# Top-k logits four heads at a time on alternating halves of the array's rows, products with values on alternating column halves

## Chip, cores and metric

The kernel runs on one core of a Trainium2 chip. The metric is device time in microseconds (us) of one execution, as the median of several runs.

## What is computed

A trunk of two layers on 256 tokens of width 1024. A layer is a root-mean-square norm, a wide projection, two attention mixers side by side (8 heads each of 64 for the top-k mixer, 4 pairs of heads for the differential one), a projection back, and a SwiGLU block. Cut to what matters here:

```python
qa, ka, va, iq, ik, iw, qb, kb, vb = split(rms_norm(x) @ w_in)
# top-k mixer: each query keeps the 64 keys with the best index score
score = sum_h relu(iq_h . ik) * iw_h ;  idx = top_k(score, 64)
logits = qa_h . ka_h[idx] / 8 ;  out_a = softmax(logits) @ va_h[idx]      # 8 heads
# differential mixer
p = softmax(qb_hc . kb_hc / 8) ;  out_b = rms_norm((p_0 - lam * p_1) @ vb_h)  # 4 heads, c = 0, 1
x = x + concat(out_a, out_b) @ w_out
x = x + (silu(h2 @ w_gate) * (h2 @ w_up)) @ w_down
```

A query sees only keys of its own and earlier chunks of 64, so the first 128 queries (block 0) see 128 keys and the second 128 (block 1) see 256.

## The kernel before, in words

Tokens lie in two blocks of 128. Each large product is made of three products of float32r parts (`mm3`, lines 193 to 199: activations' hi by weights' hi, lo by hi, hi by lo). The weights come by DMA as `wraw` and are split on chip: ScalarE (ACT) casts `whi` (line 174), VectorE (DVE) subtracts to `wlo` (line 175). Activations are split the same way: `split_psum` casts `hi` on ACT (L303, or L306 with a gain) and makes `lo` on DVE (L304, L307).

The order of TensorE (PE) is written out by the class `Weave`. There is one main stream of large products: seven groups of the projection (idx, qb, kb, vb, qa, ka, va), then `wo`, then gate, up and down. Beside it run threads of small work, generators that yield a delay and a list of events. `small_mm`, `transpose` and `mm3` add an estimated time to `W.now` (`W.spend`), and a thread goes on in front of the main stream once its delay has passed and its events are there. So an estimate that changes moves all that is planned after it. The other engines' order is set by the tile scheduler, which follows program order and readiness. PSUM is eight banks, taken in turn.

The threads that matter here: `attn_b` (diff mixer; logits `lg_b`, transposed probabilities `ppt_b` and `pT_b`, output `ob`, its norm `subln` that ends in `pt_mb`, `hi_mb`, `lo_mb`), `attn_a` (top-k mixer; `lg_a`, `ppt_a`, `pT_a`) and `pv_a` (products with values, output `po`, split to `hi_ma`, `lo_ma`). `wo` reads first `hi_mb`, `lo_mb` of both blocks, then `hi_ma`, `lo_ma`.

A head's query and key have 64 rows, so a logit matmul takes half of the array's rows: even heads the rows 0 to 63, odd heads 64 to 127. `softmax_pair` does two heads of one half into one bank: two matmuls, on DVE a masked row-maximum for each head (L479), on ACT the exponential (L482), on DVE the reciprocal of the sums (L485). `attn_a` asks for pairs (0, 2), (1, 3), (4, 6), (5, 7) of a block, up to three ahead of the transposes; `attn_b` calls it twice in a row, for the two pairs of an item. An output `po` is 64 columns of values by 128 queries, so its matmul takes half of the array's columns; block 1 adds two key tiles.

Of the kernel before, what the change touches and what calls it, by code (L numbers as in the profile page):

```python
# [17 lines left out]
P = 128  # L18
D = 1024
S = 256  # L20
# [28 lines left out]
class Weave:  # L49
    """Orders the tensor engine's work: one main stream of large products, and threads of small  # L50
    ones, each of which says how long (in estimated microseconds) its operands take to be ready."""

# [56 lines left out]
def tile_hybrid_trunk(ctx, tc, x, w_in, w_out, vecs, w_gate, w_up, w_down, g_final, rope, out):  # L109
# [10 lines left out]

    # ---------------------------------------------------------------- weight stream
    NSUB = 1024
# [81 lines left out]

    # ---------------------------------------------------------------- inputs that stay
    LAMROW = 2 * DEPTH * KT + DEPTH
# [28 lines left out]

    # gains and lambda vectors, one per column
    gT = pool.tile([P, ROWS], F32, tag="gT", name="gT")
# [57 lines left out]
    def split_psum(pt, name, scales=None, tag="act", bufs=12):  # L295
        """Columns of a bank as hi and lo tiles; scales: one factor per partition for each of them."""
        n = pt.shape[1]
        tags = tag if isinstance(tag, tuple) else (tag, tag)
        bufs = bufs if isinstance(bufs, list) else [bufs, bufs]
        hi = pool.tile([P, 4, P], F32R, tag=tags[0], bufs=bufs[0], name=f"hi_{name}")  # L300
        lo = pool.tile([P, 4, P], F32R, tag=tags[1], bufs=bufs[1], name=f"lo_{name}")
        if scales is None:
            nc.scalar.copy(hi[:, :n], pt)  # L303
            nc.vector.tensor_tensor(lo[:, :n], pt, hi[:, :n].bitcast(F32), op=ALU.subtract)  # L304
        elif len(scales) == 1:
            nc.scalar.activation(hi[:, :n], pt, AF.Copy, scale=scales[0])  # L306
            nc.vector.scalar_tensor_tensor(lo[:, :n], pt, scales[0], hi[:, :n].bitcast(F32),  # L307
                                           op0=ALU.mult, op1=ALU.subtract)
        else:
            sc = pool.tile([P, 4, P], F32, tag="hff", bufs=3, name=f"sc_{name}")  # L310
            for k in range(0, n, 2):
                scaled(sc, pt, scales, k, k + 2)
                hilo(sc, hi, lo, k, k + 2)
        return [(hi[:, k], lo[:, k]) for k in range(n)]
# [32 lines left out]
    def norm(kind, L, b, h):  # L347
        """One half of the transposes of x, scaled by the gain (the row factor is applied to the products)."""
        yield DN, ()
        norm_T(kind, L, b, h)  # L350
        norm_split(kind, L, b, h)
        if h == 1:
            rstd[kind, L, b] = norm_rstd(b, f"{kind}{L}{b}")

    # ---------------------------------------------------------------- what follows a projection
    T = {}

    def matT(t, o, name):
        """[tokens, 512] -> [128, 4, tokens], float32."""
        pt = bank(f"ptq_{name}").rearrange("p (k t) -> p k t", k=4)  # L360
        for k in range(4):
            transpose(pt[:, k], t[:, k * P:(k + 1) * P])
        nc.scalar.copy(o, pt)
# [17 lines left out]
    def after_proj(L, nm, b, ps):  # L381
        name = f"{nm}{L}{b}"
        r = rstd["mix", L, b]
        if nm == "idx":
# [5 lines left out]
            nc.vector.tensor_tensor(t.rearrange("p h d -> p (h d)"), a[:, :288], c[:, :288], op=ALU.add)  # L390
            # hi and lo side by side: (hi, lo, hi, lo) of a query meets (hi, hi, lo, lo) of a key
            sq = pool.tile([P, 8, 4, 32], F32R, tag=("kbT", "kaT")[b], bufs=1, name=f"ixq{L}{b}")
# [36 lines left out]

    # ---------------------------------------------------------------- attention  # L430
    def small_mm(cost, *a, **k):
        nc.tensor.matmul(*a, **k)  # L432
        W.spend(cost)
# [32 lines left out]

    def softmax_pair(L, b, q, k, mask, pair, name):
        """Unnormalized probabilities of two heads of one row group, and one over their sums."""
        nk = (b + 1) * P
        ps = bank(f"lg_{name}").rearrange("p (i k) -> p i k", i=2)  # L470
        for i, h in enumerate(pair):
            rws = slice(64 * (h % 2), 64 * (h % 2) + 64)
            small_mm(0.213 * (b + 1), ps[:, i, :nk], T[q, b][rws, h // 2, :], T[k][rws, h // 2, :nk],
                     start=True, stop=True)
        p = pool.tile([P, 2, S], F32, tag="prob", bufs=5, name=f"p_{name}")
        mx = small(2, f"mx_{name}")
        sm = small(2, f"sm_{name}")
        for i in range(2):
            nc.vector.tensor_tensor_reduce(out=p[:, i, :nk], in0=ps[:, i, :nk], in1=mask[:, :nk], scale=-0.125,  # L479
                                           scalar=3.0e38, op0=ALU.add, op1=ALU.min, accum_out=mx[:, i:i + 1])  # L480
        for i in range(2):
            nc.scalar.activation(p[:, i, :nk], p[:, i, :nk], AF.Exp, scale=-1.0, bias=mx[:, i:i + 1],  # L482
                                 accum_out=sm[:, i:i + 1])
        rc = small(2, f"rc_{name}")
        nc.vector.reciprocal(rc, sm)  # L485
        return p, rc

# [9 lines left out]
    def attn_b(L):  # L497
# [5 lines left out]
        def qk(b, hp):  # L503
            nk = (b + 1) * P
            p0, r0 = softmax_pair(L, b, "qb", "kb", smask[:, b], (4 * hp, 4 * hp + 2), f"b{L}{b}{hp}0")
            p1, r1 = softmax_pair(L, b, "qb", "kb", smask[:, b], (4 * hp + 1, 4 * hp + 3), f"b{L}{b}{hp}1")
            nl = small(2, f"nl{L}{b}{hp}")
            nc.vector.tensor_scalar(nl, r1, neglam[:, L:L + 1], None, op0=ALU.mult)
            for i in range(2):
                nc.scalar.activation(p1[:, i, :nk], p1[:, i, :nk], AF.Copy, scale=nl[:, i:i + 1])  # L510
                nc.vector.scalar_tensor_tensor(p0[:, i, :nk], p0[:, i, :nk], r0[:, i:i + 1], p1[:, i, :nk],
                                               op0=ALU.mult, op1=ALU.add)
            prob[b, hp] = p0
            ready[b, hp] = W.now + DB[b]
# [41 lines left out]
    def attn_a(L):  # L556
        items = [(b, n) for b in range(NB) for n in range(4)]
        ready, prob, pTs = {}, {}, {}

        def qk(b, n):  # L560
            nk = (b + 1) * P
            p, rc = softmax_pair(L, b, "qa", "ka", T["mask", b], PAIRS[n], f"a{L}{b}{n}")
            for i in range(2):
                nc.vector.tensor_scalar(p[:, i, :nk], p[:, i, :nk], rc[:, i:i + 1], None, op0=ALU.mult)
            prob[b, n] = p
            ready[b, n] = W.now + DA[b]

        nq = 0
        for n, (b, pr) in enumerate(items):
            while nq < min(n + AHEAD + 1, len(items)):  # L570
                yield (DQA if nq else 0.0), tuple((m, L, i) for m in ("qa", "ka") for i in range(items[nq][0] + 1))
                qk(*items[nq])
                nq += 1
            yield max(0.0, ready[b, pr] - W.now), ()
            pTs[b, pr] = probT(prob[b, pr], b, f"a{L}{b}{pr}", f"pT{b}", 4)
            if pr == 3:
                W.done(("pta", L, b), 1.2)
                W.spawn(pv_a(L, b, [pTs[b, i] for i in range(4)]))

    def pv_a(L, b, pTs):  # L580
        yield 0, (("pta", L, b),) + tuple(("va", L, i) for i in range(b + 1))
        po = bank(f"po{L}{b}").rearrange("p (h q) -> p h q", h=4)
        for pair, pT in zip(PAIRS, pTs):
            for i, h in enumerate(pair):
                for kt in range(b + 1):
                    small_mm(0.213, po[64 * (h % 2):64 * (h % 2) + 64, h // 2, :], T["va", kt][:, h * 64:(h + 1) * 64],
                             pT[:, i, kt], start=(kt == 0), stop=(kt == b))
        T["mixa", b] = split_psum(po, f"ma{L}{b}")
        W.done(("mixa", L, b), 1.8)

    # ---------------------------------------------------------------- the feed-forward block
    ffT = {}
# [15 lines left out]

    # ---------------------------------------------------------------- the main stream
    def group(kind, L, key, n, first, after):  # L610
        """act @ w for both blocks; first: the acts are only being made, so one block after the other."""
        banks = [bank(f"ps_{key[1]}{L}{key[2] if len(key) > 2 else ''}{b}") for b in range(NB)]
# [95 lines left out]
    def final(b, cuts, gfin):  # L708
        """The last norm of one block, piece by piece as its columns come."""
        n = len(cuts)  # L710
# [28 lines left out]
    def startup(after):  # L739
        n = NCOL["idx"]  # L740
        with tc.manual_schedule(engines={ENG.Activation, ENG.DVE}):
# [15 lines left out]

            # the first block in plain float32, which waits for no splitting
            first = [begin(0, h) for h in range(2)]
# [85 lines left out]
```

## Time and profile before

| | before |
|---|---|
| median of 3 runs | 647.33 us (646.92 to 649.78) |
| profiled execution (told by its span) | 645.0 us |
| PE busy | 635.2 us, 98% |
| DVE busy | 437.9 us, 68% |
| ACT busy | 365.2 us, 57% |
| granted PE clock, tenths of full | 9 in each of 40 slices |

The profile is one execution of its own. Its span runs from the first to the last recorded instruction and is 2.3 us below the median of the timed runs. Busy time is a share of that span. A PE row gives its start, and a length that reaches to the modelled end of the last of its records; since matmuls are pipelined, two neighbours overlap, and the distance between starts is what one costs in a row. A matmul of two float32 operands appears as two records. Rows of DVE and ACT can end with the idle time ahead of them and what released them.

### The profile page before, as it was taken

Reading aid. Unit: us, or ns where it says so; the run is one execution under the profiler, and the core shown is the slowest. Engines: PE = TensorE matmul, PEld = TensorE weight load, DVE = VectorE, ACT = ScalarE, POOL = GpSimd, SP = SyncE. Lnnn points to the kernel's source line nnn. Section 1 sums busy time; section 2 is a strip of 40 time slices with the busy share of each in tenths; the row PEclk is TensorE's granted clock in tenths of the full one; section 3 lists DMA queues with packets and bytes.
Section 4 is the critical chain, followed back from the end, with each engine's and each line's share of the span. In section 5 each row is a group of like instructions: output and inputs, shape, how many; then the busy total and the mean of one; then the engine's idle time right before and its main releaser. Section 6 shows DMA issues by size and latency. Waiting matters only on the chain.

```text
span 645.0 us, 8819 instructions
## 1 busy us (share of the span) xinstructions
PE 635.2 (98%) x3256; PEld 526.5 (82%) x3256; DVE 437.9 (68%) x922; ACT 365.2 (57%) x636; POOL 1.9 (0%) x12
## 2 busy tenths in 40 slices
PE   8999999999999999999999999999999999999995
PEld 5888787888888889888898888778888888898885
DVE  6899997596456555544598999866765455464445
ACT  7868586675544454333487678765744554443322
POOL 1000000000000000000000000000000000000000
PEclk9999999999999999999999999999999999999999
DMA  9773453326555655555276533323655555555501
GB/s 317 228 227 101 133 187 136 131 90 236 188 168 170 197 193 196 175 191 162 69 262 203 188 131 132 132 65 131 215 180 193 195 196 166 197 163 193 196 34 65
DMA packets 49907, 108.59 MB, mean 168 GB/s; under 512 B 1826, under 2 KB 8520, under 8 KB 49864
## 3 DMA queue, kind: packets, MB, share of 16 engines
q1 hardware_dynamic: 49392, 106.96, 49.6%
q10 hardware_dynamic: 472, 1.07, 0.5%
q8 instruction: 25, 0.41, 0.3%
q14 instruction: 18, 0.15, 0.1%
HBM read 106.97 MB, written 1.05 MB: 167 GB/s over the span
## 4 chain that ended last, share of the span: by engine, by line
PE 97%; DMA 1%; DVE 0%; SPq 0%; ACT 0%; issue 0%; ACTq 0%
PE ps_gate L196 6%; PE ps_gate L198 6%; PE dn L196 6%; PE dn L197 6%; PE dn L198 6%; PE ps_gate L197 6%; PE ps_up L198 6%; PE ps_up L196 6%; PE ps_up L197 6%; PE wo L198 2%; PE wo L196 2%; PE wo L197 2%; PE lg_a L432 2%; PE pth L202 1%; PE ps_va L196 1%; PE ps_vb L196 1%
## 5 line engine op out<-in xcount | busy, mean ns | idle before, releaser
L175 DVE TENSOR_TENSOR wlo<-wraw,whi 128x1024 fp32r<-128x1024 f32 (+1 forms) x204 | 244.5, 1205 | 141.9 <-ACT whi L174 138.4
L174 ACT CAST whi<-wraw 128x1024 fp32r<-128x1024 f32 (+1 forms) x204 | 209.6, 1040 | 150.8 <-PE dn L197 50.0
L196 PE MATMUL ps_gate<-whi,hi_ffn 128*128 128x512 f32 (+1 forms) x192 | 73.7, 384 | 0.0
L196 PE MATMUL dn<-whi,hi_ff 128*128 128x512 f32 (+1 forms) x198 | 73.2, 370 | 0.0
L197 PE MATMUL dn<-whi,lo_ff 128*128 128x512 f32 (+1 forms) x198 | 72.7, 367 | 0.0
L198 PE MATMUL dn<-wlo,hi_ff 128*128 128x512 f32 (+1 forms) x198 | 72.5, 366 | 0.0
L198 PE MATMUL ps_gate<-wlo,hi_ffn 128*128 128x512 f32 (+1 forms) x192 | 71.7, 373 | 0.0
L198 PE MATMUL ps_up<-wlo,hi_ffn 128*128 128x512 f32 (+1 forms) x192 | 71.4, 372 | 0.0
L197 PE MATMUL ps_up<-whi,lo_ffn 128*128 128x512 f32 (+1 forms) x192 | 71.4, 372 | 0.0
L196 PE MATMUL ps_up<-whi,hi_ffn 128*128 128x512 f32 (+1 forms) x192 | 71.4, 372 | 0.0
L197 PE MATMUL ps_gate<-whi,lo_ffn 128*128 128x512 f32 (+1 forms) x192 | 71.4, 372 | 0.0
L198 PEld LDWEIGHTS dn<-wlo,hi_ff 128*128 128x128 f32 x198 | 37.3, 188 | 6.2
L196 PEld LDWEIGHTS dn<-whi,hi_ff 128*128 128x128 f32 x198 | 37.4, 189 | 5.9
L197 PEld LDWEIGHTS dn<-whi,lo_ff 128*128 128x128 f32 x198 | 37.4, 189 | 5.8
L198 PEld LDWEIGHTS ps_gate<-wlo,hi_ffn 128*128 128x128 f32 x192 | 36.1, 188 | 6.6
L197 PEld LDWEIGHTS ps_up<-whi,lo_ffn 128*128 128x128 f32 x192 | 36.2, 189 | 6.2
L198 PEld LDWEIGHTS ps_up<-wlo,hi_ffn 128*128 128x128 f32 x192 | 36.2, 188 | 6.2
L196 PEld LDWEIGHTS ps_up<-whi,hi_ffn 128*128 128x128 f32 x192 | 36.2, 189 | 6.2
L197 PEld LDWEIGHTS ps_gate<-whi,lo_ffn 128*128 128x128 f32 x192 | 36.3, 189 | 5.7
L196 PEld LDWEIGHTS ps_gate<-whi,hi_ffn 128*128 128x128 f32 x192 | 36.2, 189 | 5.5
L303 ACT CAST hi_ff<-pth 128x512 fp32r<-128x512 f32 (+1 forms) x24 | 13.1, 544 | 20.0 <-PE pth L202 20.0
L304 DVE TENSOR_TENSOR lo_ff<-pth,hi_ff 128x512 fp32r<-128x512 f32 (+1 forms) x24 | 15.5, 645 | 8.9 <-ACT hi_ff L303 8.9
(320 smaller groups left out, 1060.8 us busy)
## 6 DMA issues: line engine op xcount, KB each, us to landing
wraw<-in_w_in_dram SPq DMA_DIRECT2D x24, 1024.0 KB, 5.1
wraw<-in_w_gate_dram SPq DMA_DIRECT2D x22, 1024.0 KB, 5.1
wraw<-in_w_up_dram SPq DMA_DIRECT2D x22, 1024.0 KB, 5.2
wraw<-in_w_down_dram SPq DMA_DIRECT2D x22, 1024.0 KB, 4.9
wraw<-in_w_out_dram SPq DMA_DIRECT2D x8, 1024.0 KB, 5.0
wraw<-in_w_in_dram SPq DMA_DIRECT2D x4, 296.0 KB, 5.0
wraw<-in_w_in_dram SPq DMA_DIRECT2D x2, 592.0 KB, 3.9
x<-in_x_dram SPq DMA_DIRECT2D x2, 256.0 KB, 3.1
```

The source lines that it names most:

```text
L174: nc.scalar.copy(hi, raw[c][:, s:s + step])
L175: nc.vector.tensor_tensor(lo, raw[c][:, s:s + step], hi.bitcast(F32), op=ALU.subtract)
L196: nc.tensor.matmul(ps, hi, whi, start=first, stop=False)
L197: nc.tensor.matmul(ps, lo, whi, start=False, stop=False)
L198: nc.tensor.matmul(ps, hi, wlo, start=False, stop=last)
L202: nc.tensor.transpose(o, i, ident)
L303: nc.scalar.copy(hi[:, :n], pt)
L304: nc.vector.tensor_tensor(lo[:, :n], pt, hi[:, :n].bitcast(F32), op=ALU.subtract)
L432: nc.tensor.matmul(*a, **k)
```

## The change

`softmax_pair` becomes `softmax_quad`: two banks, one for each pair, and four logit matmuls that take a head of the one pair and of the other in turn, so that the halves of the rows alternate; then the same softmax steps for the one pair and the other. The estimated cost of a matmul falls from 0.213 to 0.107 for 128 keys. `attn_b` makes one such call in place of two. `attn_a` has two items of four heads for a block in place of four of two, asks for one ahead, and holds the second pair's transposes back until 1.6 times the delay. `pv_a` takes two pairs at a time and alternates between them, which are on opposite column halves; its estimate falls to 0.107 too. Comments and docstrings go. Lines behind `softmax_quad` move by six or seven.

```diff
-    def softmax_pair(L, b, q, k, mask, pair, name):
+    def softmax_quad(L, b, q, k, mask, pairs, name):
         nk = (b + 1) * P
-        ps = bank(f"lg_{name}").rearrange("p (i k) -> p i k", i=2)
-        for i, h in enumerate(pair):
-            rws = slice(64 * (h % 2), 64 * (h % 2) + 64)
-            small_mm(0.213 * (b + 1), ps[:, i, :nk], T[q, b][rws, h // 2, :], T[k][rws, h // 2, :nk],
-                     start=True, stop=True)
-        p = pool.tile([P, 2, S], F32, tag="prob", bufs=5, name=f"p_{name}")
-        mx = small(2, f"mx_{name}")
-        sm = small(2, f"sm_{name}")
+        banks = [bank(f"lg_{name}{j}").rearrange("p (i k) -> p i k", i=2) for j in range(2)]
         for i in range(2):
-            nc.vector.tensor_tensor_reduce(out=p[:, i, :nk], in0=ps[:, i, :nk], in1=mask[:, :nk], scale=-0.125,
-                                           scalar=3.0e38, op0=ALU.add, op1=ALU.min, accum_out=mx[:, i:i + 1])
-        for i in range(2):
-            nc.scalar.activation(p[:, i, :nk], p[:, i, :nk], AF.Exp, scale=-1.0, bias=mx[:, i:i + 1],
-                                 accum_out=sm[:, i:i + 1])
-        rc = small(2, f"rc_{name}")
-        nc.vector.reciprocal(rc, sm)
-        return p, rc
+            for j in range(2):
+                h = pairs[j][i]
+                rws = slice(64 * (h % 2), 64 * (h % 2) + 64)
+                small_mm(0.107 * (b + 1), banks[j][:, i, :nk], T[q, b][rws, h // 2, :], T[k][rws, h // 2, :nk],
+                         start=True, stop=True)
+        out = []
+        for j in range(2):
+            p = pool.tile([P, 2, S], F32, tag="prob", bufs=5, name=f"p_{name}{j}")
+            mx = small(2, f"mx_{name}{j}")
+            sm = small(2, f"sm_{name}{j}")
+            for i in range(2):
+                nc.vector.tensor_tensor_reduce(out=p[:, i, :nk], in0=banks[j][:, i, :nk], in1=mask[:, :nk], scale=-0.125,
+                                               scalar=3.0e38, op0=ALU.add, op1=ALU.min, accum_out=mx[:, i:i + 1])
+            for i in range(2):
+                nc.scalar.activation(p[:, i, :nk], p[:, i, :nk], AF.Exp, scale=-1.0, bias=mx[:, i:i + 1],
+                                     accum_out=sm[:, i:i + 1])
+            rc = small(2, f"rc_{name}{j}")
+            nc.vector.reciprocal(rc, sm)
+            out.append((p, rc))
+        return out
...
-            p0, r0 = softmax_pair(L, b, "qb", "kb", smask[:, b], (4 * hp, 4 * hp + 2), f"b{L}{b}{hp}0")
-            p1, r1 = softmax_pair(L, b, "qb", "kb", smask[:, b], (4 * hp + 1, 4 * hp + 3), f"b{L}{b}{hp}1")
+            (p0, r0), (p1, r1) = softmax_quad(L, b, "qb", "kb", smask[:, b],
+                                              ((4 * hp, 4 * hp + 2), (4 * hp + 1, 4 * hp + 3)), f"b{L}{b}{hp}")
...
-        items = [(b, n) for b in range(NB) for n in range(4)]
+        items = [(b, n) for b in range(NB) for n in range(2)]
         ready, prob, pTs = {}, {}, {}
 
         def qk(b, n):
             nk = (b + 1) * P
-            p, rc = softmax_pair(L, b, "qa", "ka", T["mask", b], PAIRS[n], f"a{L}{b}{n}")
-            for i in range(2):
-                nc.vector.tensor_scalar(p[:, i, :nk], p[:, i, :nk], rc[:, i:i + 1], None, op0=ALU.mult)
-            prob[b, n] = p
-            ready[b, n] = W.now + DA[b]
+            for pr, (p, rc) in zip((2 * n, 2 * n + 1),
+                                   softmax_quad(L, b, "qa", "ka", T["mask", b], PAIRS[2 * n:2 * n + 2], f"a{L}{b}{n}")):
+                for i in range(2):
+                    nc.vector.tensor_scalar(p[:, i, :nk], p[:, i, :nk], rc[:, i:i + 1], None, op0=ALU.mult)
+                prob[b, pr] = p
+                ready[b, pr] = W.now + DA[b] * (1 if pr % 2 == 0 else 1.6)
 
         nq = 0
-        for n, (b, pr) in enumerate(items):
-            while nq < min(n + AHEAD + 1, len(items)):
+        for n, (b, qd) in enumerate(items):
+            while nq < min(n + 2, len(items)):
                 yield (DQA if nq else 0.0), tuple((m, L, i) for m in ("qa", "ka") for i in range(items[nq][0] + 1))
                 qk(*items[nq])
                 nq += 1
-            yield max(0.0, ready[b, pr] - W.now), ()
-            pTs[b, pr] = probT(prob[b, pr], b, f"a{L}{b}{pr}", f"pT{b}", 4)
-            if pr == 3:
+            for pr in (2 * qd, 2 * qd + 1):
+                yield max(0.0, ready[b, pr] - W.now), ()
+                pTs[b, pr] = probT(prob[b, pr], b, f"a{L}{b}{pr}", f"pT{b}", 4)
+            if qd == 1:
                 W.done(("pta", L, b), 1.2)
                 W.spawn(pv_a(L, b, [pTs[b, i] for i in range(4)]))
 
     def pv_a(L, b, pTs):
         yield 0, (("pta", L, b),) + tuple(("va", L, i) for i in range(b + 1))
         po = bank(f"po{L}{b}").rearrange("p (h q) -> p h q", h=4)
-        for pair, pT in zip(PAIRS, pTs):
-            for i, h in enumerate(pair):
+        for g in range(2):
+            for i in range(2):
                 for kt in range(b + 1):
-                    small_mm(0.213, po[64 * (h % 2):64 * (h % 2) + 64, h // 2, :], T["va", kt][:, h * 64:(h + 1) * 64],
-                             pT[:, i, kt], start=(kt == 0), stop=(kt == b))
+                    for j in range(2):
+                        h, pT = PAIRS[2 * g + j][i], pTs[2 * g + j]
+                        small_mm(0.107, po[64 * (h % 2):64 * (h % 2) + 64, h // 2, :],
+                                 T["va", kt][:, h * 64:(h + 1) * 64], pT[:, i, kt], start=(kt == 0), stop=(kt == b))
```

PE, first layer, va projection at the first top-k logits (`ps_va` the projection, `lg_a` logits, `ob` the diff mixer's output). Before:

```order
L432 MATMUL lg_a_1175<-kaT_1134,qa00T 128x128 x2
L196 MATMUL ps_va_1082<-whi_2_1090,hi_mix_126 128x512
L197 MATMUL ps_va_1082<-whi_2_1090,lo_mix_127 128x512
L198 MATMUL ps_va_1082<-wlo_2_1091,hi_mix_126 128x512
L432 MATMUL ob_1107<-vb_749,pT_b_1128 128x128
L432 MATMUL ob_1107<-vb_805,pT_b_1128 128x128
L432 MATMUL ob_1107<-vb_749,pT_b_1128 128x128
L432 MATMUL ob_1107<-vb_805,pT_b_1128 128x128
L432 MATMUL lg_a_1196<-kaT_1134,qa00T 128x128 x2
```

After:

```order
L432 MATMUL lg_a_1175<-kaT_1147,qa00T 128x128
L432 MATMUL lg_a_1176<-kaT_1147,qa00T 128x128
L432 MATMUL lg_a_1175<-kaT_1147,qa00T 128x128
L432 MATMUL lg_a_1176<-kaT_1147,qa00T 128x128
L196 MATMUL ps_va_1082<-whi_2_1090,hi_mix_126 128x512
L197 MATMUL ps_va_1082<-whi_2_1090,lo_mix_127 128x512
L198 MATMUL ps_va_1082<-wlo_2_1091,hi_mix_126 128x512
```

The two pairs stood apart, with a product step and the four matmuls of `ob` between them; now the four heads stand in a row and alternate between two banks.

PE, first layer, the end of the block-1 products with values (`po`), up to the first `wo` step that reads their split, `hi_ma_1538` before and `hi_ma_1560` after. Before:

```order
L432 MATMUL po_1521<-pT_a_1508,va_1290 64x128
L202 MATMUL pt_ffn_1542<-ident,x_62 128x128 x4
L196 MATMUL wo_1272<-whi_1_1329,hi_ma_1415 128x512
L197 MATMUL wo_1272<-whi_1_1329,lo_ma_1416 128x512
L198 MATMUL wo_1272<-wlo_1_1330,hi_ma_1415 128x512
L196 MATMUL wo_1272<-whi_0_1480,hi_ma_1415 128x512
L197 MATMUL wo_1272<-whi_0_1480,lo_ma_1416 128x512
L198 MATMUL wo_1272<-wlo_0_1481,hi_ma_1415 128x512
L196 MATMUL wo_1272<-whi_1_1484,hi_ma_1415 128x512
L197 MATMUL wo_1272<-whi_1_1484,lo_ma_1416 128x512
L198 MATMUL wo_1272<-wlo_1_1485,hi_ma_1415 128x512
L196 MATMUL wo_1273<-whi_0_1325,hi_ma_1538 128x512
```

After:

```order
L432 MATMUL po_1543<-pT_a_1501,va_1304 64x128
L432 MATMUL po_1543<-pT_a_1515,va_1304 64x128
L196 MATMUL wo_1286<-whi_1_1470,hi_ma_1429 128x512
L197 MATMUL wo_1286<-whi_1_1470,lo_ma_1430 128x512
L198 MATMUL wo_1286<-wlo_1_1471,hi_ma_1429 128x512
L196 MATMUL wo_1287<-whi_0_1320,hi_ma_1560 128x512
L197 MATMUL wo_1287<-whi_0_1320,lo_ma_1561 128x512
L198 MATMUL wo_1287<-wlo_0_1321,hi_ma_1560 128x512
```

Four transposes and six of the nine products that stood between the last `po` and that step are gone from there.

DVE, second layer, up to the blend of the diff mixer's probabilities (`p_b`, x2) that the transposes `ppt_b` read (`wlo` weight splits, `ov` and `or10` the norm of the block before). Before:

```order
L485 RECIPROCAL rc_b_3869<-sm_b_3864 128x2
L419 TENSOR_TENSOR rp_qa_3884<-rp_qa_3884,rp_qa_3886 128x512
L508 TENSOR_SCALAR nl_3871<-rc_b_3869,neglam 128x2
L175 TENSOR_TENSOR wlo_2_3959<-wraw_3791,whi_2_3958 128x1024
L511 SCALAR_TENSOR_TENSOR p_b_3850<-p_b_3850,rc_b_3857,p_b_3862 128x256 x2
```

After:

```order
L547 TENSOR_REDUCE ov_3920<-osq_3919 128x4
L175 TENSOR_TENSOR wlo_0_4042<-wraw_3837,whi_0_4041 128x1024
L490 RECIPROCAL rc_b_3879<-sm_b_3874 128x2
L548 TENSOR_SCALAR ov_3920<-ov_3920 128x4
L175 TENSOR_TENSOR wlo_2_4046<-wraw_3837,whi_2_4045 128x1024
L514 TENSOR_SCALAR nl_3881<-rc_b_3879,neglam 128x2
L271 TENSOR_SCALAR or10h<-ov_3920 128x4
L273 TENSOR_SCALAR or10y_3926<-ov_3920 128x4
L274 TENSOR_SCALAR or10y_3926<-or10y_3926 128x4
L280 TENSOR_TENSOR or10t_3929<-or10y_3926 128x4
L281 TENSOR_TENSOR or10t_3929<-or10t_3929,or10h 128x4
L517 SCALAR_TENSOR_TENSOR p_b_3863<-p_b_3863,rc_b_3870,p_b_3872 128x256 x2
```

The weight splits `wlo_0_4042` and `wlo_2_4046`, the reduction `ov` and six short steps of the norm now stand ahead of the blend.

## Rows read from the trace of the kernel before

**Rows 1.** Chain that ended last, shares of the span by engine:

```profile
PE 97%; DMA 1%; DVE 0%; SPq 0%; ACT 0%; issue 0%; ACTq 0%
```

**Rows 2.** PE's waits: line waited for: us in total, times, longest:

```profile
PE warmup L247 <- DVE warm L220: 1.2, 1, 1.2
...
```

**Rows 3.** Timeline of PE: start us, us, engine line operation out<-in xcount:

```profile
97.86 0.39 PE L198 MATMUL ps_va<-wlo,hi_mix 128*128 128x512 f32 x1
98.18 0.71 PE L432 MATMUL lg_a<-kaT,qa00T 64*128 64x128 f32 x4
98.82 0.50 PE L196 MATMUL ps_va<-whi,hi_mix 128*128 128x512 f32 x1
99.16 0.39 PE L197 MATMUL ps_va<-whi,lo_mix 128*128 128x512 f32 x1
99.39 0.40 PE L198 MATMUL ps_va<-wlo,hi_mix 128*128 128x512 f32 x1
...
105.11 1.13 PE L432 MATMUL lg_a<-kaT,qa01T 64*128 64x256 f32 x4
106.17 0.44 PE L202 MATMUL ppt_a<-ident,p_a 128*128 128x128 f32 x2
```

**Rows 4.** Timeline of PE, the diff mixer's logits:

```profile
54.10 0.72 PE L432 MATMUL lg_b<-kbT,qb00T 64*128 64x128 f32 x8
...
68.64 1.14 PE L432 MATMUL lg_b<-kbT,qb01T 64*128 64x256 f32 x8
```

**Rows 5.** Timeline of PE, products with values; then po's weight loads (ns min/median/max):

```profile
112.23 1.15 PE L432 MATMUL po<-pT_a,va 128*64 128x128 f32 x16
113.31 0.66 PE L202 MATMUL ppt_a<-ident,p_a 128*128 128x128 f32 x4
...
439.75 2.57 PE L432 MATMUL po<-pT_a,va 128*64 128x128 f32 x32
442.25 0.66 PE L202 MATMUL pt_ffn<-ident,x 128*128 128x128 f32 x4
...
L432 PEld LDWEIGHTS po<-pT_a,va x96: 132/137/138, 112.2 to 441.9; 128*64 128x64 f32 x96
```

**Rows 6.** Timeline of ACT and DVE behind po ([idle before <-releaser]):

```profile
442.36 0.59 ACT L303 CAST hi_ma<-po 128x512 fp32r<-128x512 f32 x1 [1.68 <-PE po L432]
442.98 0.69 DVE L304 TENSOR_TENSOR lo_ma<-po,hi_ma 128x512 fp32r<-128x512 f32 x1 [3.12 <-ACT hi_ma L303]
```

**Rows 7.** Second layer's projections: windows row, then timeline of DVE and PE:

```profile
352.00:407.00 55.00, 55.00 (x290) 44.83 (x290) 53.26 (x162) 41.72 (x87) 0.00 (x0) 1.00 0.43 143
...
392.75 0.87 DVE L511 SCALAR_TENSOR_TENSOR p_b<-p_b,rc_b,p_b 128x256 f32<-128x256 f32 x2
393.54 0.68 DVE L541 TENSOR_REDUCE ov<-osq 128x4 f32<-128x512 f32 x1
394.13 1.22 DVE L175 TENSOR_TENSOR wlo<-wraw,whi 128x1024 fp32r<-128x1024 f32 x1
395.27 0.16 DVE L542 TENSOR_SCALAR ov<-ov 128x4 f32<-128x4 f32 x1
395.34 0.42 DVE L479 CUSTOM_DVE_ANT_0 p_b<-lg_b,smask 128x256 f32<-128x256 f32 x1
...
394.47 0.60 PE L202 MATMUL ppt_b<-ident,p_b 128*128 128x128 f32 x4
```

**Rows 8.** Timeline of DVE and ACT behind a block-1 burst:

```profile
106.28 0.42 DVE L479 CUSTOM_DVE_ANT_0 p_a<-lg_a,amask 128x256 f32<-128x256 f32 x1 [0.45 <-PE lg_a L432]
106.64 0.37 ACT L494 COPY pT_a<-ppt_a 128x256 f32<-128x256 f32 x1 [1.01 <-PE ppt_a L202]
106.91 0.51 ACT L482 ACTIVATE p_a<-p_a,mx_a 128x256 f32<-128x256 f32 x1
107.42 0.68 ACT L306 ACTIVATE hi_mb<-pt_mb,gT 128x512 fp32r<-128x512 f32 x1
108.13 0.75 DVE L307 SCALAR_TENSOR_TENSOR lo_mb<-pt_mb,gT,hi_mb 128x512 fp32r<-128x512 f32 x1 [0.68 <-ACT hi_mb L306]
```

## The prediction

> **What bounds the kernel now.** I read first the chain of work that ended last, by engine: TensorE (PE) holds 97% of the span [rows 1]. Then the waits of PE: there are four, all in the start-up, and the longest, on the warm-up, is 1.2 us [rows 2]. So from the start-up to the end PE always has its next instruction ready, and the time is the sum of the steps from one PE start to the next. The timeline of PE gives these steps. Between two products of the main stream (512 columns) it is 99.39 - 99.16 = 0.23 us [rows 3]. An edit is therefore worth what it takes out of these steps, less every wait that it creates. VectorE (DVE) is the engine to watch for such waits: through the second layer's projections it is busy 53.26 of 55.00 us, at a granted clock of 1.00 for PE [rows 7]. The profiled span is 645.0 us and the median of the runs 647.33; I make the sum against the span and add the 2.3 us between them.
>
> **Top-k logits, the gain.** Before, each pair of heads is one burst of two matmuls on one half of the rows; both are fp32, and the trace has two records for each, so a pair shows as x4. With 128 keys a burst takes 98.82 - 98.18 = 0.64 us to the next start, with 256 keys 106.17 - 105.11 = 1.06 us [rows 3]. What two pairs cost when they stand together on opposite halves is in the same trace: that is how the diff mixer's logits (lg_b) already run, and their eight records last 0.72 us with 128 keys and 1.14 with 256 [rows 4], where the four of lg_a last 0.71 and 1.13 [rows 3]. Eight cost 0.01 more than four, so the two halves work at the same time, and a quad should take 0.65 and 1.07 to the next start. A layer has four pairs of each length for lg_a, two quads after: 4 x 0.64 - 2 x 0.65 = 1.26 and 4 x 1.06 - 2 x 1.07 = 2.10, together 3.36. Two layers: **-6.7 us**.
>
> **Diff logits, nothing.** They get the new order of heads too, but two pairs already take the time of one [rows 4]. The number and length of their matmuls stay: 0. The bounds are -2.2 (the rival of strict order, below) and a burst that falls apart into two pairs (4 x 0.64 + 4 x 1.06 = +6.8 over both layers); I take 0, since these rows are the very case.
>
> **Products with values (po), a gain.** Block 0 has 8 matmuls (x16), block 1 has 16 (x32); they take 113.31 - 112.23 = 1.08 and 442.25 - 439.75 = 2.50 us [rows 5]. Before, the order stays on one column half for four matmuls in block 1, for two in block 0, and the halves can meet only where it changes. Entering and leaving a burst of small matmuls costs 0.32 - 0.23 = 0.09 and 0.34 - 0.23 = 0.11, so 0.20 [rows 3]. Block 0 then is 0.88 / 16 = 0.055 us a record, block 1 2.30 / 32 = 0.072. If alternation gives block 1 that rate, it is 32 x 0.055 + 0.20 = 1.96, a gain of 0.54 a layer: **-1.1 us**. Block 0 is at the rate already: 0. The bounds are 0 (block 1 stays) and 1.5 (block 0 gets faster in proportion, 0.2 a layer); I take 1.1, as block 0 alternates in twos already and shows what that gives. The Trainium skill speaks against this term: "TensorE: Matmul & The Clock Gate", Part 3, says that a weight load overlaps running matmuls only where the row group differs, and column halves share their rows; by it the gain would be 0 and the forecast 1.1 us higher. The trace does not agree: a weight load of po takes 0.137 us [rows 5], and block 0 passes a record, with its load, in 0.055, so loads of the two halves do overlap.
>
> **Fewer breaks of the main stream, a gain.** Counting in the order of PE's instructions, the main stream is broken for small work 100 times before and 95 after, since four pairs became two quads and other small work falls beside them. Each break costs the 0.20 of entry and exit: **-1.0 us** (0.8 to 1.4, by what stands next to what). The gains sum to 6.7 + 1.1 + 1.0 = 8.8.
>
> **New waits.** The order of PE changes everywhere after the first cheaper logit, because the estimated costs move the plan's clock. I compared every place where PE reads what ACT or DVE makes, old slack against new order. Three lose their cover.
> First, in each layer, the split of po of block 1. The cast hi_ma starts 442.36 - 442.25 = 0.11 after the burst, lo_ma ends at 442.98 + 0.69 = 443.67, 1.42 after it [rows 6]. Before, four transposes and nine products stand ahead of its first reader. After, three products do: 0.34 + 2 x 0.23 = 0.80, and the lo half is read one product later, at 1.03. So PE waits 0.39, with some 0.05 for the signal (half of the 0.11 above, an estimate) 0.45, twice: **+0.9**. Behind it in PE's queue stands the whole w_out stream, so nothing fills it.
> Second, in each layer, lo_mb of block 1 (the diff mixer's output). From the start of the block-1 quad ahead of it the chain is: 106.28 - 105.11 = 1.17 to its first row-maximum, 106.91 - 106.28 = 0.63 to the exponential, two of these at 0.51, two copies of pT at 106.91 - 106.64 = 0.27, 108.13 - 107.42 = 0.71 for hi_mb and 0.75 for lo_mb [rows 3, 8]: 4.82. PE meanwhile does that quad (1.07), four transposes of probabilities and four of the mixer's output (8 x 0.115, from the 0.66 of four less 0.20 [rows 5], 0.92), a second quad (1.07), po of block 0 (1.08) and a first product (0.34): 4.48. ACT can run the copies earlier, so I take 0.2 a layer: **+0.4** (0 to 1.2).
> Third, in layer 1, the last blend of the diff probabilities (p_b), which four transposes read. Before, the blend ends at 392.75 + 0.87 = 393.62 and is read at 394.47: 0.85 to spare [rows 7]. After, DVE has two more weight splits (395.27 - 394.13 = 1.14 each), a reduction (394.13 - 393.54 = 0.59) and six short operations (395.34 - 395.27 = 0.07 each) ahead of it: 3.29. PE has six more products ahead: 1.36. 3.29 - 0.85 - 1.36 = **+1.1** (0.7 with one of the splits half hidden, 1.6 with short ones at their full 0.16). The other readers keep over 0.3 us.
> Waits: 0.9 + 0.4 + 1.1 = 2.4 (0 if ACT and DVE slip earlier, since PE is what they follow; 5 if each doubles). **Sum: 645.0 - 8.8 + 2.4 = 638.6 span, and with 2.3 a time of 640.9 us.**
>
> **Rivals.**
> *No wait appears.* The scheduler's order is one thing, the run another: if the splits of weights run ahead by what PE gains elsewhere, the three covers hold. 647.3 - 8.8 = 638.5. For it: PE waited for nothing before [rows 2]. Against: DVE has 1.7 us to spare in 55 [rows 7].
> *DVE becomes the bound in the projections.* PE now asks for split weights 4 us sooner a layer, and DVE at 97% cannot give them. The waits then double, 4.8: 643.3. For it: [rows 7]. Against: only the third wait lies there; ahead of lo_ma, in the attention stage, DVE stood idle for 3.12 us [rows 6].
> *The change doesn't do what it says: alternating matmuls run one after another.* Then A is gone and the splits' waits mostly with it (0.9 stays): 647.3 - 2.1 + 0.9 = 646.1. Against: lg_b [rows 4].
> *Strict order.* If matmuls could only start in the order of the program, lg_b before (both matmuls of a half, then both of the other) could overlap only in its middle: three steps where alternation needs two. Alternating would then give a third of its burst, 0.21 four times and 0.35 four times, 2.2 us more: 638.7. Against: lg_b already costs what one pair costs [rows 4]. The Trainium skill states such a rule, matmuls strictly first in, first out, in the same Part 3 of "TensorE: Matmul & The Clock Gate"; the rows on lg_b speak against it for two row halves.
> *Slower: each change of half drains the array.* Eight lg_a quads change half three times each (24), eight lg_b quads twice more than before (16), po 4 and 12 times more in each layer (32): 72 changes. At the 0.20 of an entry and exit [rows 3] that is 14.4, and with no gain from overlap 647.3 - 1.0 + 14.4 = 660.7. It decides from 6.4 / 72 = 0.09 us a change. Against: the bursts of lg_b and of po's block 0 hold changes of half already, at no visible price [rows 4, 5].
>
> **How the numbers follow.** Forecast 640.9, chance 0.60; no waits 638.5, 0.15; waits doubled 643.3, 0.13; strict order 638.7, 0.04; serial 646.1, 0.04; drains 660.7, 0.04. The range leaves the last two out, and takes in the bounds of the waits and of po on both sides: 637.8 to 644.4. A measurement of this kernel can tell about 0.5% from no change, 3.2 us, so faster means under 644.1: nearly all of the first case, all of the second and fourth, three quarters of the third: 0.87. Within: 0.09, slower: 0.04.
>
> **What the profile after would show.** Right: lg_a as x8 bursts of 0.65 and 1.07 us to the next start, lg_b unchanged, po of block 1 near 1.96, and PE waits on lo_ma, lo_mb and p_b of 0.4, 0.2 and 1.1 us. Wrong: an x8 burst of lg_a near 1.3 or 2.1 (no overlap), lg_b bursts shorter than before (strict order), po of block 1 at 2.5, or PE waits on whi or wlo in many places (DVE the bound).

## The result and the profile after

The changed kernel takes 641.75 us (median of 4 runs, 641.29 to 642.19), the kernel before beside it 647.35. The ratio is 0.991 with an interval of 0.9896 to 0.9924: 5.6 us faster. The prediction was 640.9, with a range of 637.8 to 644.4. The profiled span is 640.4 us.

The chain that ended last, by engine, beside [rows 1]. PE has lost 11 points, nine of them to DVE:

```profile
PE 86%; DVE 9%; ACT 2%; issue 1%; DMA 1%; SPq 0%; ACTq 0%
```

This is not a kernel bound by DVE. The chain is followed back through whatever released each step, so a short wait, on `p_b` at 394 us or on `kaT` at 94 us, is enough to lead it into the queues of DVE and ACT for a long stretch ahead. The waits of PE tell the size. Before, there were four, all in the start-up: the one of [rows 2] and the first three rows here. From 45 us to the end there was none before; the changed kernel has six, in the last four rows (line waited for: us in total, times, longest):

```profile
PE pt_mix L202 <- DMA x<-in_x_dram: 0.9, 1, 0.9
PE ps_idx L766 <- ACT sc_mix L289: 0.8, 1, 0.8
PE ps_idx L197 <- DVE lo_mix L293: 0.3, 1, 0.3
...
PE ppt_b L202 <- DVE p_b L517: 1.0, 1, 1.0
PE wo L197 <- DVE lo_ma L304: 0.4, 2, 0.2
PE wo L197 <- DVE lo_mb L307: 0.3, 2, 0.2
PE lg_a L432 <- ACT kaT L363: 0.3, 1, 0.3
```

The timeline of PE has the top-k logits as bursts of eight records, beside the fours of [rows 3]: 98.37 - 97.73 = 0.64 and 108.35 - 107.28 = 1.07 us to the next start. Twice as many logits pass in the time of one pair.

```profile
97.73 0.71 PE L432 MATMUL lg_a<-kaT,qa00T 64*128 64x128 f32 x8
98.37 0.50 PE L196 MATMUL ps_va<-whi,hi_mix 128*128 128x512 f32 x1
...
107.28 1.14 PE L432 MATMUL lg_a<-kaT,qa01T 64*128 64x256 f32 x8
108.35 0.66 PE L202 MATMUL ppt_a<-ident,p_a 128*128 128x128 f32 x4
108.84 0.60 PE L202 MATMUL pt_mb<-ident,on 128*128 128x128 f32 x4
109.37 1.13 PE L432 MATMUL lg_a<-kaT,qa01T 64*128 64x256 f32 x8
110.44 1.09 PE L432 MATMUL po<-pT_a,va 128*64 128x128 f32 x16
111.46 0.51 PE L196 MATMUL wo<-whi,hi_mb 128*128 128x512 f32 x1
```

The last two rows, and the ones below, stand beside [rows 5]: the products with values of block 0 take 1.02 us (1.08 before), those of block 1 take 438.78 - 436.88 = 1.90 (2.50 before). The diff mixer's logits are 0.64 and 1.06 us, as before [rows 4]:

```profile
54.85 0.71 PE L432 MATMUL lg_b<-kbT,qb00T 64*128 64x128 f32 x8
55.49 0.50 PE L196 MATMUL ps_vb<-whi,hi_mix 128*128 128x512 f32 x1
...
69.38 1.13 PE L432 MATMUL lg_b<-kbT,qb01T 64*128 64x256 f32 x8
70.44 0.44 PE L202 MATMUL ppt_b<-ident,p_b 128*128 128x128 f32 x2
```

What a wait costs is more than its row in the view of waits. Here is the one on `lo_ma` in the second layer, with ACT and DVE, beside [rows 6]:

```profile
436.88 1.97 PE L432 MATMUL po<-pT_a,va 128*64 128x128 f32 x32
438.78 0.50 PE L196 MATMUL wo<-whi,hi_ma 128*128 128x512 f32 x1
...
439.58 0.46 PE L196 MATMUL wo<-whi,hi_ma 128*128 128x512 f32 x1
440.26 0.50 PE L197 MATMUL wo<-whi,lo_ma 128*128 128x512 f32 x1 [0.22 <-DVE lo_ma L304]
440.60 0.40 PE L198 MATMUL wo<-wlo,hi_ma 128*128 128x512 f32 x1
...
438.90 0.59 ACT L303 CAST hi_ma<-po 128x512 fp32r<-128x512 f32 x1 [0.76 <-PE po L432]
...
439.52 0.69 DVE L304 TENSOR_TENSOR lo_ma<-po,hi_ma 128x512 fp32r<-128x512 f32 x1 [0.45 <-ACT hi_ma L303]
```

`lo_ma` is there at 439.52 + 0.69 = 440.21 and PE goes on at 440.26. The view of waits counts 0.22, since the product that began at 439.58 still shows as busy. But the step from 439.58 to the next start is 440.26 - 439.58 = 0.68, where it is 0.23 without a wait [rows 3], and the first step behind it is 0.34 in place of 0.23: 0.56 us lost. The others, in the same way:

```profile
423.74 0.50 PE L196 MATMUL wo<-whi,hi_mb 128*128 128x512 f32 x1
424.41 0.50 PE L197 MATMUL wo<-whi,lo_mb 128*128 128x512 f32 x1 [0.16 <-DVE lo_mb L307]
424.74 0.40 PE L198 MATMUL wo<-wlo,hi_mb 128*128 128x512 f32 x1
...
393.15 0.40 PE L198 MATMUL ps_ka<-wlo,hi_mix 128*128 128x512 f32 x1
394.56 0.83 PE L202 MATMUL ppt_b<-ident,p_b 128*128 128x128 f32 x4 [1.01 <-DVE p_b L517]
395.15 0.48 PE L196 MATMUL ps_ka<-whi,hi_mix 128*128 128x512 f32 x1
...
93.73 0.60 PE L202 MATMUL pt_mb<-ident,on 128*128 128x128 f32 x4
94.61 0.60 PE L432 MATMUL lg_a<-kaT,qa00T 64*128 64x128 f32 x6 [0.28 <-ACT kaT L363]
```

`lo_mb`: 0.67 where the step behind a burst is 0.34, and 0.33 for 0.23, so 0.43. `p_b`: 1.41 for 0.23, and 0.59 for the four transposes where they take 0.35 without a wait, so 1.42. `kaT`: 0.88 from the first transpose to the logits, where the same four take 109.37 - 108.84 = 0.53 above, so 0.35. With two layers for the first two: 2 x 0.56 + 2 x 0.43 + 1.42 + 0.35 = **3.75 us of waits**.

Spans of single profiles need one correction. Up to the first logits of the diff mixer, every kernel of this study has the same instructions on PE, DVE and ACT, yet these logits start at 50.52 us in the profile of before and at 51.31 in that of after (up to 52.06 in others): the start-up varies from run to run. Counted from there to PE's end, after is 5.4 us shorter, in agreement with the timed 5.6. Summed over all PE starts from there on, lg_a gives -6.74, po -1.31, lg_b -0.05 and the waits above +3.75; the rest, -1.1, is what is left for the five breaks less of the main stream. Below, what is said to be in the trace is such a sum over all starts.

### The profile page after: what moved, and what is told of

It reads as the page before. It is cut to its first block, busy times and chain, and to the rows that moved or that the text cites. A ratio compares the mean times of both kernels' runs of the same rounds, so it can differ in the third digit from the quotient of the medians.

```text
span 640.4 us, 8817 instructions
## 1 busy us (share of the span) xinstructions
PE 628.8 (98%) x3256; PEld 521.8 (81%) x3256; DVE 436.8 (68%) x922; ACT 365.4 (57%) x636; POOL 1.9 (0%) x12
## 3 DMA queue, kind: packets, MB, share of 16 engines
q10 hardware_dynamic: 472, 1.07, 0.4%
HBM read 106.97 MB, written 1.05 MB: 169 GB/s over the span
## 4 chain that ended last, share of the span: by engine, by line
PE 86%; DVE 9%; ACT 2%; issue 1%; DMA 1%; SPq 0%; ACTq 0%
PE ps_gate L198 6%; PE ps_gate L196 6%; PE dn L196 6%; PE dn L197 6%; PE dn L198 6%; PE ps_gate L197 6%; PE ps_up L198 6%; PE ps_up L196 6%; PE ps_up L197 6%; PE wo L197 2%; PE wo L198 2%; PE wo L196 2%; DVE wlo L175 2%; PE pth L202 2%; PE ps_kb L196 1%
## 5 line engine op out<-in xcount | busy, mean ns | idle before, releaser
L487 ACT ACTIVATE p_b<-p_b,mx_b 128x128 f32<-128x128 f32 (+1 forms) x32 | 14.4, 451 | 12.5 <-DVE mx_b L484 11.9
```

## Experiments

Each kernel was timed in several rounds against the kernel before on the same chip (647.40 beside the three that change the kernel before and the one with one factor of the plan moved, 647.27 beside the others).

**Is it the alternation?** The changed kernel, with the two heads of a pair issued together again, one pair behind the other:

```diff
-        for i in range(2):
-            for j in range(2):
+        for j in range(2):
+            for i in range(2):
                 h = pairs[j][i]
```

> The changed kernel, but the four logit matmuls of a quad are issued pair by pair (two on the one half of the rows, then two on the other) in place of alternating; the plan and all else stay. Theory (what counts is that opposite halves stand next to each other; PE takes them side by side in either order): the eight-record bursts stay at 0.65 and 1.07 us and the time at 641.8, within 0.4. Rival (the alternation itself counts, matmuls start only in program order): each of the 16 bursts grows by a third to a half, 0.2 to 0.5 us, and the time is 645 to 648.

642.20 us (641.62 to 644.1), ratio 0.9922 (0.9909 to 0.9935), against 0.991 for the changed kernel. The bursts stay (97.77 - 97.12 = 0.65, 107.76 - 106.69 = 1.07):

```profile
97.12 0.72 PE L432 MATMUL lg_a<-kaT,qa00T 64*128 64x128 f32 x8
97.77 0.50 PE L196 MATMUL ps_va<-whi,hi_mix 128*128 128x512 f32 x1
...
106.69 1.14 PE L432 MATMUL lg_a<-kaT,qa01T 64*128 64x256 f32 x8
107.76 0.44 PE L202 MATMUL ppt_a<-ident,p_a 128*128 128x128 f32 x2
```

For the logits the alternation is worth nothing that can be measured; it is enough that both pairs stand in one place.

**Is it the two halves?** The changed kernel, with all top-k logits on the first half of the rows (the logits of odd heads are then those of even ones):

```diff
-                rws = slice(64 * (h % 2), 64 * (h % 2) + 64)
+                half = h % 2 if q == "qb" else 0
+                rws = slice(64 * half, 64 * half + 64)
```

> The changed kernel, but the top-k mixer's logits all read rows 0 to 63 of queries and keys, so its quads sit on one half of the rows; the logits of odd heads are then those of even ones, which changes the computation but not its amount. The plan stays. Theory (the gain is from two halves at work at the same time): lg_a bursts grow to about 1.28 and 2.12 us, twice the burst of a pair, so 4 x 0.63 + 4 x 1.06 = 6.8 us more, less some 0.6 of the wait on lo_mb that they now cover: 647.9. Rival (the gain is from fewer breaks and the new plan, not from the halves): the bursts grow little, 642 to 643.

646.17 us (645.24 to 646.95), ratio 0.9978 (0.9969 to 0.9987). That is 4.4 above the changed kernel, where 6.2 were expected. The timeline says why:

```profile
97.51 1.16 PE L432 MATMUL lg_a<-kaT,qa00T 64*128 64x128 f32 x8
98.60 0.50 PE L196 MATMUL ps_va<-whi,hi_mix 128*128 128x512 f32 x1
...
107.51 1.99 PE L432 MATMUL lg_a<-kaT,qa01T 64*128 64x256 f32 x8
109.43 0.66 PE L202 MATMUL ppt_a<-ident,p_a 128*128 128x128 f32 x4
```

A serial quad takes 1.09 and 1.92, not 1.28 and 2.12: twice the burst of a pair counts its entry and exit (0.2) twice. So of the 6.74 us on lg_a, 4 x (1.09 - 0.64) + 4 x (1.92 - 1.07) = 5.2 come from the two halves at work at once, and 1.5 from one burst where there were two. The waits on `lo_mb` are gone in this kernel, since the longer quads cover them, which gives 0.9 back: 5.2 - 0.9 = 4.3, near the 4.4 measured. The rows also tell what one half is busy with. Less entry and exit, a record takes (1.09 - 0.20) / 8 = 0.111 us with 128 keys and (1.92 - 0.20) / 8 = 0.215 with 256, while its weight load takes 0.188 and 0.187 in this run: the time goes with the columns that stream through, not with the load.

**The products with values, alone and undone.** Undone in the changed kernel:

```diff
-        for g in range(2):
-            for i in range(2):
+        for pair, pT in zip(PAIRS, pTs):
+            for i, h in enumerate(pair):
                 for kt in range(b + 1):
-                    for j in range(2):
-                        h, pT = PAIRS[2 * g + j][i], pTs[2 * g + j]
```

> The changed kernel with the products with values in the old order, pair by pair, at the new estimate, so that the plan stays. Theory (alternating column halves let weight loads and passes overlap): po goes back from 1.02 to 1.08 and from 1.90 to 2.50 us, 0.65 a layer, and the time is 643.0. Rival (po is followed by waits that absorb it, the split of its result is what PE waits for): 641.8.

643.18 us (643.08 to 643.43), ratio 0.9931 (0.9919 to 0.9943): 1.4 above the changed kernel, as the theory has it. Done alone, in the kernel before, with the reverse of this edit and the estimate left at 0.213:

> The kernel before, with the products with values alternating column halves as the changed kernel does, at the old estimate of their cost, so that the plan is that of before. Theory: po goes from 1.08 to 1.02 and from 2.50 to 1.90 us, 0.65 a layer; before, the splits of its result had cover, so all of it comes through: 1.3 us less than before, 646.0. Rival (weight loads of two column halves don't overlap any more than they do): 647.3.

645.94 us (645.46 to 646.76), ratio 0.9978 (0.9970 to 0.9986): 1.5 below. In its timeline the two bursts are 114.48 - 113.46 = 1.02 and 128.47 - 126.57 = 1.90, and PE waits for nothing new:

```profile
113.46 1.09 PE L432 MATMUL po<-pT_a,va 128*64 128x128 f32 x16
114.48 0.66 PE L202 MATMUL ppt_a<-ident,p_a 128*128 128x128 f32 x4
...
126.57 1.97 PE L432 MATMUL po<-pT_a,va 128*64 128x128 f32 x32
128.47 0.66 PE L202 MATMUL pt_ffn<-ident,x 128*128 128x128 f32 x4
```

So here, other than for the logits, the order inside the burst counts. Why one and not the other? The next kernel takes the order of before to its other end: all heads of one column half, then all of the other, in the kernel before.

```diff
-        for pair, pT in zip(PAIRS, pTs):
+        for pair, pT in [(PAIRS[n], pTs[n]) for n in (0, 2, 1, 3)]:
```

> The kernel before, with the products with values taking all heads of the one column half first and then all of the other (pairs in the order 0, 2, 1, 3), at the old estimate. Theory (PE reaches only a few instructions ahead, so halves overlap only where they stand close): most of the burst is serial at 0.109 us a record, block 0 near 1.6 and block 1 near 3.4 us, 1.4 us a layer more than before: 650.1 (649 to 651). Rival (PE reaches far ahead, or the order doesn't count): the bursts stay at 1.08 and 2.50 us, 647.3.

649.84 us (649.36 to 651.57), ratio 1.004 (1.0024 to 1.0056), and bursts of 114.37 - 112.86 = 1.51 and 129.71 - 126.45 = 3.26:

```profile
112.86 1.58 PE L432 MATMUL po<-pT_a,va 128*64 128x128 f32 x16
114.37 0.66 PE L202 MATMUL ppt_a<-ident,p_a 128*128 128x128 f32 x4
...
126.45 3.33 PE L432 MATMUL po<-pT_a,va 128*64 128x128 f32 x32
129.71 0.55 PE L202 MATMUL pt_ffn<-ident,x 128*128 128x128 f32 x3
...
126.45 1.52 PE L432 MATMUL po<-pT_a,va 128*64 128x128 f32 x12
```

The last row is the same burst up to 127.80: twelve of the sixteen records of the first half start alone, 0.11 us apart. The records' starts go on with eight in a mixed stretch up to 128.30, about 0.055 us apart, and twelve alone to the end. So exactly the last four records of the one half run beside the first four of the other. Four records are two fp32 matmuls: in this burst PE reaches that far ahead, and no farther. It fits all bursts here. Logits pair by pair change half after two matmuls, within the reach: no loss. Products of block 0 changed half after two as well: 1.08, against 1.02 alternating. Products of block 1 changed after four: 2.50 against 1.90. With halves apart only the middle overlaps. For the halves of the rows the reach itself is not shown: no run put them more than two matmuls apart.

**The diff mixer's logits alone.** In the kernel before, `attn_b` with one call of `softmax_quad` at the old estimate:

```diff
-            p0, r0 = softmax_pair(L, b, "qb", "kb", smask[:, b], (4 * hp, 4 * hp + 2), f"b{L}{b}{hp}0")
-            p1, r1 = softmax_pair(L, b, "qb", "kb", smask[:, b], (4 * hp + 1, 4 * hp + 3), f"b{L}{b}{hp}1")
+            (p0, r0), (p1, r1) = softmax_quad(L, b, "qb", "kb", smask[:, b],
+                                              ((4 * hp, 4 * hp + 2), (4 * hp + 1, 4 * hp + 3)), f"b{L}{b}{hp}")
```

> The kernel before, with only the diff mixer's logits taken four at a time on alternating halves, at the old estimate, so that the plan is that of before. Theory (two pairs on opposite halves already run side by side): no change, bursts of 0.65 and 1.07 us, 647.3 within 0.4. Rival (strict order of starts): bursts a third shorter, 645.1.

647.26 us (646.62 to 648.56), ratio 0.9999 (0.9990 to 1.0008): nothing. In the trace the steps of lg_b sum to 6.84 us, 6.89 before.

**The waits.** One factor of the plan alone, in the changed kernel:

```diff
-                ready[b, pr] = W.now + DA[b] * (1 if pr % 2 == 0 else 1.6)
+                ready[b, pr] = W.now + DA[b] * (1 if pr % 2 == 0 else 1.4)
```

> The changed kernel with one factor of the plan moved: the second pair's transposes of a quad come after 1.4 in place of 1.6 times the delay. In the order that results, the readers of lo_mb and lo_ma stand behind what covers them, and the blend p_b stays as late as in the changed kernel. Theory: the waits on lo_mb (0.33 a layer over its normal step) and lo_ma (0.45) go, 1.5 us in all, less some 0.8 of breaks that come with the new order: PE waits on p_b alone, and the time is 641.0 (640.2 to 641.4). Rival (a wait that is taken away comes back at the next thing that is late): 641.8, with a wait in another place of the attention stage.

639.76 us (639.36 to 641.02), ratio 0.9883 (0.9869 to 0.9898): 2.0 below the changed kernel, more than expected. Of PE's waits behind the start-up two are left, on `p_b` (1.0) and `kaT` (0.3), as they were. The prices of those that went, read from the steps above with the slow step behind each wait, are 2 x 0.56 + 2 x 0.43 = 1.98; the expectation had left that step out, and had charged breaks at 0.8. From the first diff logits to PE's end its trace is 2.0 us shorter than the changed kernel's as well, so the two breaks that this plan has more cost nothing in sum. All four delays moved:

```diff
-DB = (8.0, 10.0)
-DA = (5.0, 6.5)
-DPV = 4.0
+DB = (8.0, 10.5)
+DA = (5.0, 5.0)
+DPV = 3.0
...
-                ready[b, pr] = W.now + DA[b] * (1 if pr % 2 == 0 else 1.6)
+                ready[b, pr] = W.now + DA[b] * (1 if pr % 2 == 0 else 1.4)
```

> The changed kernel with four of the plan's delays moved: block 1's transposes of the top-k mixer 5.0 in place of 6.5 after its logits and the second pair's factor 1.4 in place of 1.6, the diff mixer's block-1 transposes 10.5 in place of 10.0, its products 3.0 in place of 4.0 after the transposes. No instruction is added or taken away. In the order that results, the readers of lo_ma, lo_mb and p_b stand later than these are ready. Theory (the waits cost what the profile shows, some 3 us): PE waits for nothing after the start-up and the time is 639.2, within 0.6. Rival (a wait that is taken away comes back at the next thing that is late): 641 to 642.

**639.42 us** (638.47 to 639.8), ratio 0.987 (0.9858 to 0.9883), the fastest here, 2.3 below the changed kernel. Its interval and that of the kernel with one factor moved overlap, so the timed runs don't tell the two apart. From 45 us to the last stores PE waits once, where no wait was expected:

```profile
PE ob L432 <- ACT pT_b L500: 0.2, 1, 0.2
...
85.23 0.39 PE L198 MATMUL ps_ka<-wlo,hi_mix 128*128 128x512 f32 x1
85.83 1.16 PE L432 MATMUL ob<-vb,pT_b 128*128 128x128 f32 x8 [0.21 <-ACT pT_b L500]
...
392.42 0.39 PE L198 MATMUL ps_ka<-wlo,hi_mix 128*128 128x512 f32 x1
392.65 0.60 PE L202 MATMUL ppt_b<-ident,p_b 128*128 128x128 f32 x4
393.00 0.48 PE L196 MATMUL ps_ka<-whi,hi_mix 128*128 128x512 f32 x1
...
352.00:407.00 55.00, 55.00 (x299) 44.63 (x297) 54.37 (x162) 41.62 (x87) 0.00 (x0) 1.00 0.44 149
```

The step into the transposes of `p_b` is 0.23 again. The last row is the window of [rows 7] in this kernel: DVE is busy 54.37 of 55.00 us and PE doesn't wait for it. A queue that full is not a bound as long as what it makes is early. From the first diff logits to PE's end this kernel is 3.1 us shorter than the changed one, not 3.75. Of the 0.65 that is missing, the wait that is left takes 0.37: the step into `ob` is 85.83 - 85.23 = 0.60 in place of 0.23. The plan also has eight breaks of the main stream more; all the other steps together come to the remaining 0.28, and what these breaks cost by themselves was not measured.

## Why the prediction was right, and where it was off

**The bound** held: the change in PE's steps, with the waits in them, is 5.4 us in the trace, and the timed change is 5.6.

**Top-k logits**: -6.7 predicted, -6.74 in the trace. The price came from a burst of the same form that the kernel already had, the diff mixer's. What the two halves gave and what one burst in place of two gave were not told apart there; the run on one half tells them apart, 5.2 and 1.5.

**Diff logits**: 0 predicted, 0 measured (ratio 0.9999).

**Products with values**: -1.1 predicted, -1.31 in the trace, and 1.4 and 1.5 in the two timed comparisons. Block 0 was put at its best rate, 0.055 us a record, and was not: its order changed half every two matmuls and had 0.06 us to lose. At the rate of the alternating order, (1.90 - 0.20) / 32 = 0.053, block 0 would be 16 x 0.053 + 0.20 = 1.05, near its 1.02.

**Breaks**: -1.0 predicted, -1.1 as the rest of the sum; no run measured this term by itself.

**Waits**: this is the term that was mis-sized, +2.4 predicted and +3.75 measured. The gains came out 0.4 larger, which by luck makes up for a part of it; what is left is about the 0.85 between 640.9 and 641.75. All three places were right. `lo_ma` was put at 0.45 and its step grew by 0.45; but behind a wait the next step is 0.34 in place of 0.23, and the sum left this out (0.11 for each of four waits). `lo_mb` was put at 0.2 and was 0.33, near the 4.82 - 4.48 = 0.34 of its own two chains, which had been shaded down on the ground that ACT could run its copies earlier. It did not: in the first layer they start at 109.92 us, behind both exponentials, which start at 108.92 and 109.42. `p_b` was put at 1.1 and was 1.18, and 0.24 more inside the four transposes behind it. The sentence that other readers keep over 0.3 us was wrong for `kaT` ahead of the first quad, which cost 0.35.

**The rivals.** That no wait appears is refuted by the four rows of waits, though the moved plan comes near it with one. That DVE is the bound is refuted by the same rows: none is on `whi` or `wlo`. That matmuls run one after another is refuted by the bursts. Of drains at a change of half nothing shows: the alternating bursts of the products with values are shorter than those with fewer changes. Strict order is refuted by the pair-by-pair run and by the diff logits alone, for which it asked changes of at least 3 and of 2 us. The rule of the Trainium skill, "TensorE: Matmul & The Clock Gate", Part 3, that matmuls start and end strictly first in, first out, does not hold for these fp32 matmuls: pair by pair, two pairs in a row take 0.65 us like alternating ones, where one pair takes 0.64. Nor does the other rule of that part of the Trainium skill, that weight loads overlap running matmuls only where the row group differs: the column halves share their rows, and po of block 1 falls to 0.053 us a record at weight loads of 0.137 [rows 5]. The overlap of loads is not what alternation adds, though: with one column half alone at work, in the run with the halves apart, a record passes every 0.11 us, less than one load of 0.137, so loads overlap running matmuls there too.

## What to carry to other kernels

Matmuls that fill half of the array should stand next to ones on the other half, no more than two fp32 matmuls apart; whether they alternate one by one or two by two matters little (0.06 us at most here), but four by four the products with values, 16 matmuls, took 2.50 us in place of 1.90. Where an engine is the bound, a faster burst takes the cover off what is made beside it: read, for each consumer in the new order, how long its operand takes and how much work stands ahead, and charge the slow step behind each wait too. If the order is planned by estimated costs, changed costs need changed delays: here that was worth another 2.3 us, without an instruction added.

## What was not expected of the hardware

PE overlaps halves out of program order, but only four records (two fp32 matmuls) across the change of column half: 12 alone, 8 mixed, 12 alone in the burst of 3.26 us.

A wait costs its time and a slow restart: the first 512-column step behind it took 0.34 us in place of 0.23, as much as behind the bursts of logits and of products with values (0.34).
